# Value products of two attention stages: a head's high and low value parts side by side as one stationary, and rows of exponentials divided by their sums

## The chip, the cores and the metric

The kernel runs on one core of a Trainium2 chip. The metric is device time in microseconds of that core; lower is better. A profile adds one execution seen by the hardware profiler, with every instruction on the five engines: TensorE (PE, whose weight loads stand apart as PEld), VectorE (DVE), ScalarE (ACT), GpSimd (POOL) and SyncE (SP), which issues the transfers.

## What is computed

A causal decoder trunk of two layers on 512 tokens of width 1024, in float32. Layer 0 mixes with 4 differential heads and 8 dilated heads; layer 1 mixes with 16 heads that see only keys picked by an indexer. Each layer then has a squared-ReLU MLP and a gated embedding. The change touches the last step of the dilated heads and of layer 1's heads, which in the reference is

```
pr = jnp.exp(s - lse[..., None])
o = jnp.einsum('bhcnqk,bhcnkd->bhcnqd', pr.astype(v.dtype), vv)
...
pr = jax.nn.softmax(jnp.where(valid[:, :, None, :], s, -jnp.inf), axis=-1)
o_lat = jnp.einsum('bqhk,bqkc->bqhc', pr.astype(sel.dtype), sel[..., :C_KV_RANK])
return jnp.einsum('bqhc,chd->bqhd', o_lat, w_uv)
```

The kernel applies `w_uv` to the keys' latent first, so that a head of layer 1 has values of 64 columns, as the dilated heads have.

## The kernel before

To keep float32 accuracy every operand of a product is split into a high part, which TensorE takes exactly, and a low part (the difference). A product is then three passes, `mm3` (L203): high by high, high by low, low by high. TensorE follows the order of the program; the other engines' orders come from a scheduler.

Both attention stages run through `head_pipe` (L404), a software pipeline over heads. Per step it issues four stages for different heads, in the order of `ORDER_B` for the dilated heads ("stage B" below, 8 heads) and `ORDER_C` for layer 1 ("stage C", 16 heads). In C, step i does A for head i+3, B for i+2, C for i and D for i-1:

- A transposes queries (tile `trq`, L381).
- B computes scores in four query tiles of 128, 256, 384 and 512 keys (tile `sc`), takes row maxima on VectorE (L346), exponentials with row sums on ScalarE (L347), written to the head's tile `p` (`pb` or `pc`, 128x1280). For the second head of a pair it takes reciprocals of the pair's eight sums (L424) and spreads them along rows (tile `rsb`). At its end the next pair's keys are split (`k_load`, tile `kc`: high part on VectorE, low part on GpSimd, L1131).
- C transposes ten 128x128 blocks of `p` (tile `trp`, L361) and splits them into a high (ScalarE, L364) and a low part (VectorE, L365).
- D is the product (tile `pv`, `pv_head` L368). The stationary of a matmul is the 128 value columns of a pair of heads, so half of the 128 output rows belong to the other head and are not used. Six groups of blocks (`GRP`) times three passes are 18 matmuls. For the first head of a pair it also transposes `rsb` on TensorE (tile `rs`, L439, four transposes) and ScalarE copies it to `rbp` (L441). VectorE multiplies product and `rbp` into the tile `on` (L446). After the second head, `on` is split into the output's high part (ScalarE) and low part (L450: GpSimd in B, VectorE in C). After the first head, the values of the next pair are split in C (`v_pair`, tile `vhl`, low part on GpSimd, L1148).

In stage B pieces of other products (`ple`, and `pj` of the output projection) follow the steps; in stage C only the last steps have such pieces. After each stage the output projection (`out_proj`, tile `pj`) goes on; its fourth piece needs the last pair's output. Scores and products share four PSUM banks (tag A).

```
    def mm3(ps, aH, aL, bH, bL, first, last):
        mm(ps, aH, bH, first, False)
        mm(ps, aH, bL, False, False)
        mm(ps, aL, bH, False, last)
```

Of the kernel before, what the change touches and what calls it, by code (L numbers as in the profile page):

```python
# [18 lines left out]
P = 128  # L19
# [16 lines left out]
# how the phases are woven: how much other work of the tensor engine follows a step of a  # L36
# pipeline, the heads that each of its stages runs ahead, the order of chunks
# [10 lines left out]
# engines: low parts of weight units (v: VectorE, p: GpSimd); spread sums, products'  # L48
# low and high parts; values' and keys' parts
# [3 lines left out]
ENG_B = ("act", "pool", "act")  # L53
ENG_C = ("pool", "vec", "act")
# [4 lines left out]
def trunk_kernel(ctx, tc, A, out):  # L59
# [3 lines left out]
    # the tensor engine runs in the order of the program  # L63
# [34 lines left out]
    # the activation functions' table is loaded before the first data come  # L98
# [5 lines left out]
    # row statistics: short-lived columns go round, kept ones stay  # L104
# [109 lines left out]
    # rows (128) of an activation in two parts, transposed: per k tile a slice  # L214
# [89 lines left out]
    # post-norm of y (two psum halves) added to the residual row tile r  # L304
# [14 lines left out]
    # pre-norm statistics of h (row tile r): 1/rms into rstd[:, r]  # L319
# [31 lines left out]
    # P (rows, per q tile at OFF) transposed into two parts, blocks ordered for the  # L351
    # products: q tiles (0,1): k0 q0 q1, k1 q1; q tiles (2,3): k0..k2 q2 q3, k3 q3
# [34 lines left out]
    def scores(qp, kk):  # L387
        """scores of the four q tiles, the first two in one bank."""
# [15 lines left out]
    def head_pipe(small, n, order, on, stA, kk, bias, scale, vHL, oHL, ptile, ptT, slack=0.0, end=0.0, done=None, scored=None):  # L404
# [3 lines left out]
        sums, inv = [None], {}  # L408
# [25 lines left out]
        def st_d(h):  # L434
            m = h % 2
            if m == 0:
                pr = bank("B", "rs")
                for qt in range(NR):
                    pe.transpose(pr[:, qt * P : (qt + 1) * P], inv[h + 1][:, qt].rearrange("p m d -> p (m d)"), ident)  # L439
                o[0] = small("rbp", h // 2), small("on", h // 2)  # L440
                act.copy(o[0][0], pr)  # L441
            rb, t = o[0]
            rows = slice(64 * m, 64 * m + 64)
            ps = bank("A", "pv")
            pv_head(ps, *vHL(h), *tr[h])
            vec.tensor_tensor(t[rows], ps[rows], rb[rows], op=ALU.mult)  # L446
            if m:
                oH, oL = oHL(h)
                cp(on[2], oH, t)
# [11 lines left out]
    def ple_proj(i, stage):  # L461
        """half of the projected embedding of layer i, through stage tiles to DRAM."""
# [18 lines left out]
    def rope_rows(mp, ps, n, half, cs, dst, leng):  # L481
        """dst = rotated ps; ps [128, n] viewed as heads of 2*half columns."""
# [12 lines left out]
    def rope32(mp, pv, heads, cs, dst, e=pool):  # L495
        """dst = rotated pv; pv [128, heads, 32]; dst the same, or [128, heads/2, 2, 32]."""
# [13 lines left out]
    def out_proj(oT):  # L510
        """the first columns of a mixer's output; its first three pieces need not the last heads."""
# [11 lines left out]
    with tc.tile_pool(name="att0", bufs=1) as mp:  # L523
# [11 lines left out]
        # chunk order: ak aq av bk bq bv (columns of w_in_ab are aq ak av bq bk bv)  # L535
# [9 lines left out]
        # first chunk: all row tiles at once, as the k tiles arrive  # L545
# [6 lines left out]
        # the tensor engine's clock comes up while the first loads are under way  # L552
# [27 lines left out]
        # statistics of x, rotation tables scaled by them  # L580
# [15 lines left out]
        # lambda  # L596
# [12 lines left out]
        # av: [kt][head, part, 128]  # L609
# [12 lines left out]
        # --- A: differential attention  # L622
# [93 lines left out]
        # --- B projections  # L716
        bk, evk = rope_evac("bk")
        bq, evq = rope_evac("bq")
        bvH = slot(5, "bvH", F32R).rearrange("p (k d) -> p k d", d=512)
        bvL = slot(9, "bvL", F32R).rearrange("p (k d) -> p k d", d=512)  # L720

        def bv_evac(r, ps):
            act.activation(bvH[:, r, :], ps, AF.Identity, scale=rstd0[:, r : r + 1])
            vec.scalar_tensor_tensor(bvL[:, r, :], ps, rstd0[:, r : r + 1], f32(bvH[:, r, :]), op0=ALU.mult, op1=ALU.subtract)
# [12 lines left out]
        # --- B: the three branches as one softmax over keys with multiplicities  # L737
# [18 lines left out]
        def small_b(nm, pr):  # L756
            return s3[:, {"rsb": pr % 2, "rbp": 2, "on": 3}[nm]]

        def v_b(h):
            c = slice(h // 2 * P, h // 2 * P + P)  # L760
            return lambda kt: bvH[:, kt, c], lambda kt: bvL[:, kt, c]
# [3 lines left out]
        weave(head_pipe(small_b, 8, ORDER_B, ENG_B, st_a, lambda h: ksets[h // 2 % 2][h % 2], lambda qt: mB[:, S - (qt + 1) * P :], SCALE_AB,  # L765
                        v_b, lambda h: (oTH[1][:, h // 2, :], oTL[1][:, h // 2, :]),
                        lambda h: (slot(1, "pb"), s4)[h % 4 - 2] if h % 4 >= 2 else mp.tile([P, 1280], F32, tag="p", bufs=2, name="pb"),
                        lambda h: pt_pair(mp, (12, 13) if h % 2 else None, f"pb{h}"), B_SLACK, B_END),
              itertools.chain(ple_proj(0, lambda q: stg[:, q % 4, :]), itertools.islice(og, 3)))
# [20 lines left out]
            # hidden layer, transposed  # L790
# [48 lines left out]
            # the projected embedding  # L839
# [3 lines left out]
            # second MLP product  # L843
# [38 lines left out]
            # gate  # L882
# [47 lines left out]
    def begin(xn):  # L930
        # the next mixer's first two row tiles, while the last one is normalised
# [6 lines left out]
    # =========================================================================  # L938
    # layer 1 mixer
    # =========================================================================  # L940
    with ExitStack() as ctx2:
# [8 lines left out]
        with tc.tile_pool(name="idx", bufs=1) as ip:  # L950
# [13 lines left out]
            def latent(ps, r, n, j, g):  # L964
                """rows of a normed latent; the transposes come later."""
# [13 lines left out]
            # queries' latent  # L979
# [11 lines left out]
            # keys' latent, rotated key, indexer key and weights  # L991
# [52 lines left out]
            # indexer queries (q tiles 1..3; the first keeps all its keys)  # L1044
# [43 lines left out]
            def queries():  # L1088
# [15 lines left out]
                # keys without the rotated part, transposed, a pair of heads each  # L1104
# [34 lines left out]
        # values of a pair of heads  # L1139
        vhl = slot(11, "vhl", F32R).rearrange("p (b t k d) -> p b t k d", b=2, t=2, k=NR)  # L1140
# [113 lines left out]
```

## Time and profile before

| | us |
|---|---|
| median of 3 runs | 1360.66 (1360.48 to 1360.87) |
| span of the profiled execution, first to last instruction | 1359.8 |
| PE busy in the span | 1342.1 (99%) |
| DVE / ACT / POOL busy | 711.0 (52%) / 576.0 (42%) / 262.4 (19%) |
| mean granted clock of TensorE | 0.997 of full speed |

The profiled execution has no time of its own beside its span; the median of the runs is 0.9 us above that span. The shares are means over a kernel with very different stages: stage B lies at about 190 to 243 us of the span, stage C at 813 to 914 us. PE at 99% says that TensorE seldom stands still, not that it is at its peak.

### The profile page before, as it was taken

The page shows a single profiled execution, that of the slowest core. Times are in us where ns is not written, and L with a number is a line of the kernel's source. Part 1 is how long each engine was busy: PE and PEld are TensorE (multiplying, and loading weights), DVE is VectorE, ACT ScalarE, POOL GpSimd, SP SyncE. Part 2 cuts the span into 40 slices and gives each one's busy share as a digit, 9 for nine tenths or more (in the row PEclk, how much of TensorE's full clock was granted, in tenths as well). Part 3 has the DMA queues.
Part 4 walks back from the last instruction along what each step waited for, and adds up shares of the span by engine and source line. Part 5 has one row for each costly group of instructions (what it writes and reads, how often), then busy time and mean ns, then how long its engine had stood idle before and what let it go on. Part 6 is the DMA issues. An engine that isn't in the chain of part 4 may idle for free.

```text
span 1359.8 us, 17867 instructions
## 1 busy us (share of the span) xinstructions
PE 1342.1 (99%) x6809; PEld 1129.8 (83%) x6809; DVE 711.0 (52%) x1297; ACT 576.0 (42%) x1113; POOL 262.4 (19%) x233
## 2 busy tenths in 40 slices
PE   9999999999999999999998999999999999999998
PEld 6888889888888888888897679998988888888887
DVE  6567677374333322225567998965633332222263
ACT  4244577244222322233355768854432223222332
POOL 4202101032000022222012753410400001222120
PEclk9999999999999999999999999999999999999999
DMA  7312131423333423332243331011432334333321
GB/s 287 106 62 71 62 117 55 155 98 120 93 103 99 155 93 98 103 94 77 94 150 101 109 112 44 1 62 64 133 100 93 95 105 157 93 93 99 103 77 48
DMA packets 40838, 135.39 MB, mean 100 GB/s; under 512 B 4656, under 2 KB 5808, under 8 KB 40752
## 3 DMA queue, kind: packets, MB, share of 16 engines
q1 hardware_dynamic: 40752, 134.24, 30.7%
q8 instruction: 54, 0.88, 0.3%
q14 instruction: 32, 0.26, 0.1%
HBM read 125.83 MB, written 8.39 MB: 99 GB/s over the span
## 4 chain that ended last, share of the span: by engine, by line
PE 89%; DVE 7%; POOL 2%; issue 1%; DMA 1%; ACT 0%; SPq 0%; POOLq 0%; DVEq 0%; ACTq 0%
PE z L201 26%; PE y L201 26%; PE pj L201 21%; PE sc L201 5%; PE pv L201 4%; PE trp L361 2%; DVE work L1085 2%; DVE m L1084 2%; PE ple L201 1%; PE ak L201 1%; POOL wl L141 1%; PE tr L242 1%; PE trq L381 1%; DVE wl L141 1%; PE pva L201 1%
## 5 line engine op out<-in xcount | busy, mean ns | idle before, releaser
L141 DVE TENSOR_TENSOR wl<-raw,wh 128x1024 fp32r<-128x1024 f32 (+3 forms) x190 | 250.4, 1322 | 276.1 <-ACT wh L137 273.9
L137 ACT CAST wh<-raw 128x1024 fp32r<-128x1024 f32 (+3 forms) x206 | 212.2, 1033 | 282.5 <-issue 184.8
L201 PE MATMUL y<-wh,ah 128*128 128x512 f32 x512 | 199.5, 390 | 0.0
L201 PE MATMUL y<-wh,al 128*128 128x512 f32 x512 | 199.2, 389 | 0.0
L201 PE MATMUL y<-wl,ah 128*128 128x512 f32 x512 | 199.2, 389 | 0.0
L201 PE MATMUL pj<-wh,big 128*128 128x512 f32 (+1 forms) x444 | 148.5, 386 | 0.0
L808 DVE SCALAR_TENSOR_TENSOR t<-z,rb 128x512 f32<-128x512 f32 x64 | 44.2, 691 | 187.2 <-PE z L201 187.2
L201 PEld LDWEIGHTS y<-wh,al 128*128 128x128 f32 x512 | 96.1, 188 | 20.0
L201 PEld LDWEIGHTS y<-wl,ah 128*128 128x128 f32 x512 | 96.1, 188 | 19.9
L201 PEld LDWEIGHTS y<-wh,ah 128*128 128x128 f32 x512 | 96.1, 188 | 19.7
L863 POOL TENSOR_TENSOR al<-big,ah 128x512 fp32r<-128x512 f32 x24 | 32.6, 1360 | 383.8 <-ACT ah L862 383.8
L201 PE MATMUL z<-hz1H,wl 128*128 128x512 f32 (+1 forms) x288 | 105.3, 366 | 0.6 <-DVE wl L141 0.6
L201 PE MATMUL z<-hz0H,wl 128*128 128x512 f32 (+1 forms) x288 | 105.3, 366 | 0.6 <-DVE wl L141 0.6
L201 PE MATMUL z<-hz1H,wh 128*128 128x512 f32 (+1 forms) x288 | 105.5, 366 | 0.2 <-ACT hz1H L248 0.2
L201 PE MATMUL z<-hz0H,wh 128*128 128x512 f32 (+1 forms) x288 | 105.5, 366 | 0.2 <-ACT hz0H L248 0.2
L201 PE MATMUL z<-hz0L,wh 128*128 128x512 f32 (+1 forms) x288 | 105.3, 366 | 0.3 <-DVE hz0L L249 0.3
L201 PE MATMUL z<-hz1L,wh 128*128 128x512 f32 (+1 forms) x288 | 105.3, 366 | 0.3 <-DVE hz1L L249 0.3
L201 PEld LDWEIGHTS pj<-wh,big 128*128 128x128 f32 x444 | 82.9, 188 | 18.9 <-issue 2.2
L862 ACT CAST ah<-a 128x512 fp32r<-128x512 f32 x40 | 24.8, 621 | 154.6 <-PE y L201 154.6
L863 POOL TENSOR_TENSOR al<-a,ah 128x512 fp32r<-128x512 f32 x40 | 51.7, 1293 | 165.9 <-ACT ah L862 165.9
L209 POOL TENSOR_TENSOR st<-st,mhalf 128x1 f32<-128x1 f32 (+1 forms) x41 | 27.6, 674 | 226.9 <-DVE st L312 115.8
L201 PEld LDWEIGHTS z<-hz1H,wl 128*128 128x128 f32 x288 | 54.3, 189 | 9.7 <-DVE wl L141 0.8
(598 smaller groups left out, 2687.2 us busy)
## 6 DMA issues: line engine op xcount, KB each, us to landing
raw<-in_w_mi_dram SPq DMA_DIRECT2D x64, 512.0 KB, 3.7
raw<-in_w_mo_dram SPq DMA_DIRECT2D x64, 512.0 KB, 3.6
raw<-in_w_ab_dram SPq DMA_DIRECT2D x20, 512.0 KB, 4.8
raw<-in_w_g_dram SPq DMA_DIRECT2D x16, 512.0 KB, 3.6
raw<-in_w_oab_dram SPq DMA_DIRECT2D x8, 512.0 KB, 4.3
ple<-ple_dram SPq DMA_DIRECT2D x8, 512.0 KB, 5.4
raw<-in_w_oc_dram SPq DMA_DIRECT2D x8, 512.0 KB, 3.6
xr<-in_x_dram SPq DMA_DIRECT2D x4, 512.0 KB, 9.5
```

The lines of the kernel that those rows point to most:

```text
L137: act.copy(h[:, :n], raw[:, :n])
L141: (pool if e == "p" else vec).tensor_tensor(l[:, c], raw[:, c], f32(h[:, c]), op=ALU.subtract)
L201: pe.matmul(ps, a, b, start=first, stop=last, skip_group_check=True)
L209: pool.tensor_tensor(dst, src, mhalf[:, :n], op=ALU.pow)
L242: pe.transpose(ps[:, i * P : (i + 1) * P], src(k), ident)
L361: pe.transpose(ps[:, i * P : (i + 1) * P], pt[:, OFF[qt] + kt * P : OFF[qt] + (kt + 1) * P], ident)
L381: pe.transpose(ps[:, r * P : (r + 1) * P], rows(r), ident)
L808: vec.scalar_tensor_tensor(t, ps, 0.0, rb, op0=ALU.max, op1=ALU.mult)
L862: act.copy(ah, src)
L863: pool.tensor_tensor(al, src, f32(ah), op=ALU.subtract)
L1084: vec.max(m8, w)
L1085: vec.match_replace(w, m8, w, MARK)
```

## The change

1. The values of a head are stored as [high 64 | low 64] (tiles `bv`, `vhl`), so one stationary holds both parts of one head, and the 128 output rows are (high part's product, low part's product). `pv_head` then needs two passes, with the high and the low part of the transposed exponentials: 12 matmuls.
2. The two halves of the output are added: ScalarE copies the low half into `on`, shifted to the head's 64 partitions, and VectorE adds the high half.
3. `rsb`, `rs` and `rbp` are gone. Each head takes reciprocals of its own four sums and GpSimd multiplies the four stretches of `p` by them, in place, before the transposes.
4. The low part of the output in stage C goes from VectorE to GpSimd (`ENG_C`), and C's `p` has three buffers in place of two. `on` has one buffer in C, as before.

```diff
-ENG_B = ("act", "pool", "act")
-ENG_C = ("pool", "vec", "act")
+ENG_B = ("act", "pool")
+ENG_C = ("act", "pool")
...
-    def pv_head(ps, vH, vL, th, tl):
+    def pv_head(ps, v, th, tl):
         for kt, b, q, w in GRP:
             o = ps[:, q * P : (q + w) * P]
-            ph, pl = th[:, b * P : (b + w) * P], tl[:, b * P : (b + w) * P]
-            mm3(o, vH(kt), vL(kt), ph, pl, b == 0, (kt == 1 and q == 1) or kt == 3)
+            mm(o, v(kt), th[:, b * P : (b + w) * P], b == 0, False)
+            mm(o, v(kt), tl[:, b * P : (b + w) * P], False, (kt == 1 and q == 1) or kt == 3)
...
-            nmx = stat(4)
-            if h % 2 == 0:
-                sums[0] = stat(8)
-            sm = sums[0][:, 4 * (h % 2) : 4 * (h % 2) + 4]
+            nmx, sm, rs = stat(4), stat(4), stat(4)
...
-            if h % 2:
-                rs = stat(8)
-                vec.reciprocal(rs, sums[0])
-                inv[h] = small("rsb", h // 2).rearrange("p (q m d) -> p q m d", q=NR, m=2)
-                cp(on[0], inv[h], rs.rearrange("p (m q) -> p q m", m=2).unsqueeze(3).to_broadcast([P, NR, 2, 64]))
+            vec.reciprocal(rs, sm)
+            for qt in range(NR):
+                c = slice(OFF[qt], OFF[qt] + (qt + 1) * P)
+                pool.tensor_scalar(t[:, c], t[:, c], rs[:, qt : qt + 1], None, op0=ALU.mult)
...
-                pr = bank("B", "rs")
-                for qt in range(NR):
-                    pe.transpose(pr[:, qt * P : (qt + 1) * P], inv[h + 1][:, qt].rearrange("p m d -> p (m d)"), ident)
-                o[0] = small("rbp", h // 2), small("on", h // 2)
-                act.copy(o[0][0], pr)
-            rb, t = o[0]
-            rows = slice(64 * m, 64 * m + 64)
+                o[0] = otile(h // 2)
+            t = o[0]
+            rows, rest = slice(64 * m, 64 * m + 64), slice(64 - 64 * m, 128 - 64 * m)
             ps = bank("A", "pv")
-            pv_head(ps, *vHL(h), *tr[h])
-            vec.tensor_tensor(t[rows], ps[rows], rb[rows], op=ALU.mult)
+            pv_head(ps, v(h), *tr[h])
+            act.copy(t[rows], ps[rest])
+            vec.tensor_tensor(t[rows], ps[rows], t[rows], op=ALU.add)
...
-                        lambda h: mp.tile([P, 1280], F32, tag="p", bufs=2, name="pc"), pt_c, 0.0, C_END,
+                        lambda h: mp.tile([P, 1280], F32, tag="p", bufs=3, name="pc"),
+                        lambda pr: mp.tile([P, S], F32, tag="on", bufs=1, name="on"), pt_c, 0.0, C_END,
```

TensorE in stage C, the first head of a pair: transposes of head 9's `p` (`trp`) and head 8's product (`pc8H`, `pc8L` are its transposed exponentials). Before:

```order
L361 MATMUL trp<-ident,pc 128x128 x10
L439 MATMUL rs<-ident,rsb 128x128 x4
L201 MATMUL pv<-pc8H,vhl 128x256
L201 MATMUL pv<-pc8L,vhl 128x256
L201 MATMUL pv<-pc8H,vhl 128x256
L201 MATMUL pv<-pc8H,vhl 128x128
L201 MATMUL pv<-pc8L,vhl 128x128
L201 MATMUL pv<-pc8H,vhl 128x128
```

With the change, the same place:

```order
L361 MATMUL trp<-ident,pc 128x128 x10
L201 MATMUL pv<-pc8H,vhl 128x256
L201 MATMUL pv<-pc8L,vhl 128x256
L201 MATMUL pv<-pc8H,vhl 128x128
L201 MATMUL pv<-pc8L,vhl 128x128
L201 MATMUL pv<-pc8H,vhl 128x256
```

Each of the six groups loses its third matmul, and the four transposes of `rs` are gone.

GpSimd in stage C, one pair of heads. Before (low parts of two keys, the spread sums, low parts of values):

```order
L1131 TENSOR_TENSOR kc<-kn_6005,kc 64x512
L73 COPY rsb<-st 128x512
L1131 TENSOR_TENSOR kc<-kn_6005,kc 64x512
L1148 TENSOR_TENSOR vhl<-v_5554,vhl 128x256
L1148 TENSOR_TENSOR vhl<-v_5555,vhl 128x256
```

With the change, also one pair:

```order
L1120 TENSOR_TENSOR kc<-kn_5973,kc 64x512
L421 TENSOR_SCALAR pc<-pc,st 128x128
L421 TENSOR_SCALAR pc<-pc,st 128x256
L421 TENSOR_SCALAR pc<-pc,st 128x384
L421 TENSOR_SCALAR pc<-pc,st 128x512
L1120 TENSOR_TENSOR kc<-kn_5973,kc 64x512
L421 TENSOR_SCALAR pc<-pc,st 128x128
L421 TENSOR_SCALAR pc<-pc,st 128x256
L421 TENSOR_SCALAR pc<-pc,st 128x384
L421 TENSOR_SCALAR pc<-pc,st 128x512
L1137 TENSOR_TENSOR vhl<-v_5522,vhl 128x4x64
L1137 TENSOR_TENSOR vhl<-v_5523,vhl 128x4x64
```

The next row there is `L442`, the low part of the output (tile `oc`). So the pair has eight multiplications and one subtraction more, and no copy; a head's multiplications stand two steps ahead of the transposes that read them.

ScalarE in stage C with the change, from the copy of head 6's product to the exponentials of head 10, with waits:

```order
L437 COPY on<-pv 64x512 [waits PE_49,Pool_49]
L384 CAST qc11H<-trq 128x512 [waits PE_49]
L364 CAST pc8H<-trp 128x512 [waits PE_49]
L347 ACTIVATE pc,st<-pc,st 128x128 [waits DVE_49]
L347 ACTIVATE pc,st<-pc,st 128x256 [waits DVE_49]
```

The copy of a pair's first head writes the single tile `on`, and so waits for GpSimd's L442 of the pair before, which stands in GpSimd's queue behind a later head's multiplications and the next values; queries and exponentials are queued behind the copy.

## Rows read from the trace of the kernel before

**Rows 1.** Busy time by engine in stage C and stage B (PE, PEld, DVE, ACT, POOL, clock)
```profile
840.00:885.80 45.80, 45.80 (x370) 44.35 (x368) 43.27 (x121) 39.35 (x113) 18.64 (x20) 1.00 0.07 24
198.50:236.10 37.60, 37.60 (x273) 33.75 (x271) 26.32 (x66) 28.37 (x74) 3.85 (x3) 1.00 0.15 54
```

**Rows 2.** Chain that ended last, stage B and its end: start us, us, what
```profile
198.69 0.44 PE rs L439 x4
199.12 2.05 PE pv L201 x18
...
240.53 0.70 DVE big L446
...
241.26 0.63 ACT oTbH L73
...
241.95 1.29 POOL oTbL L450
...
243.29 6.87 PE pj L201 x29
```

**Rows 3.** The same chain in stage C
```profile
863.16 2.05 PE pv L201 x18
...
874.63 2.05 PE pv L201 x18
...
903.97 1.09 PE trp L361 x10
905.50 2.05 PE pv L201 x18
907.55 1.42 PE pj L201 x6
```

**Rows 4.** Timeline of PE in one product of stage C, in part
```profile
863.41 0.28 PE L201 MATMUL pv<-pc6L,vhl 128*128 128x128 f32 x1
863.53 0.44 PE L201 MATMUL pv<-pc6H,vhl 128*128 128x128 f32 x2
863.81 0.28 PE L201 MATMUL pv<-pc6L,vhl 128*128 128x256 f32 x1
863.92 0.40 PE L201 MATMUL pv<-pc6H,vhl 128*128 128x256 f32 x2
864.16 0.28 PE L201 MATMUL pv<-pc6L,vhl 128*128 128x256 f32 x1
```

**Rows 5.** Groups of GpSimd by form, whole span: busy us, mean ns
```profile
L1131 POOL TENSOR_TENSOR kc<-kn,kc 64x512 fp32r<-64x512 f32 x16 | 20.6, 1288 | 32.7 <-DVE kc L73 21.8 <-PE sc L201 11.0
...
L1080 POOL TENSOR_TENSOR work<-rl,work 128x384 f32<-128x384 f32 x7 | 7.1, 1013 | 3.3 <-ACT rl L1079 3.0
...
L450 POOL TENSOR_TENSOR oTbL<-big,oTbH 128x512 fp32r<-128x512 f32 x4 | 5.1, 1287 | 67.5 <-ACT oTbH L73 67.5
...
L73 POOL COPY rsb<-st 128x512 f32<-128x512 f32 x8 | 5.0, 623 | 15.7 <-DVE st L424 15.5
```

**Rows 6.** GpSimd's lines L593 and L1148: duration ns min/median/max
```profile
L593 POOL TENSOR_SCALAR cs<-cs,st x4: 522/524/1439, 24.4 to 26.8; 128x96 f32<-128x96 f32 x4
...
L1148 POOL TENSOR_TENSOR vhl<-v,vhl x16: 727/735/1457, 795.9 to 895.6; 128x256 fp32r<-128x256 f32 x16
```

**Rows 7.** Timeline of GpSimd and VectorE at the start of stage C
```profile
819.56 1.30 POOL L1131 TENSOR_TENSOR kc<-kn,kc 64x512 fp32r<-64x512 f32 x1 [10.99 <-PE sc L201]
...
822.40 1.28 POOL L1131 TENSOR_TENSOR kc<-kn,kc 64x512 fp32r<-64x512 f32 x1 [1.54 <-DVE kc L73]
...
821.84 0.42 DVE L73 CAST kc<-kn 64x512 fp32r<-64x512 f32 x1
...
823.33 0.64 DVE L73 CAST kc<-kn 64x512 fp32r<-64x512 f32 x1
```

**Rows 8.** Groups of VectorE and ScalarE by form, 840 to 885.8 us
```profile
L450 DVE TENSOR_TENSOR oc<-on,oc 128x512 fp32r<-128x512 f32 x5 | 4.0, 802 | 0.7
...
L441 ACT COPY rbp<-rs 128x512 f32<-128x512 f32 x4 | 2.5, 618 | 0.0
```

More of the change, by code (lines that the diff above doesn't have):

```diff
@@ L402, in pt_pair, with head_pipe @@
                 mp.tile([P, 1280], F32R, tag="ptl", bufs=1, name=name + "L"))
-    def head_pipe(small, n, order, on, stA, kk, bias, scale, vHL, oHL, ptile, ptT, slack=0.0, end=0.0, done=None, scored=None):
+    def head_pipe(n, order, on, stA, kk, bias, scale, v, oHL, ptile, otile, ptT, slack=0.0, end=0.0, done=None, scored=None):
         q, p, tr, o = {}, {}, {}, [None]
-        sums, inv = [None], {}
         def st_a(h):
@@ L436, in st_d @@
             if m == 0:
-                pr = bank("B", "rs")
-                for qt in range(NR):
-                    pe.transpose(pr[:, qt * P : (qt + 1) * P], inv[h + 1][:, qt].rearrange("p m d -> p (m d)"), ident)
-                o[0] = small("rbp", h // 2), small("on", h // 2)
-                act.copy(o[0][0], pr)
-            rb, t = o[0]
-            rows = slice(64 * m, 64 * m + 64)
+                o[0] = otile(h // 2)
+            t = o[0]
+            rows, rest = slice(64 * m, 64 * m + 64), slice(64 - 64 * m, 128 - 64 * m)
             ps = bank("A", "pv")
-            pv_head(ps, *vHL(h), *tr[h])
-            vec.tensor_tensor(t[rows], ps[rows], rb[rows], op=ALU.mult)
+            pv_head(ps, v(h), *tr[h])
+            act.copy(t[rows], ps[rest])
+            vec.tensor_tensor(t[rows], ps[rows], t[rows], op=ALU.add)
             if m:
                 oH, oL = oHL(h)
-                cp(on[2], oH, t)
+                cp(on[0], oH, t)
                 eng[on[1]].tensor_tensor(oL, t, f32(oH), op=ALU.subtract)
@@ L718, in trunk_kernel @@
         bq, evq = rope_evac("bq")
-        bvH = slot(5, "bvH", F32R).rearrange("p (k d) -> p k d", d=512)
-        bvL = slot(9, "bvL", F32R).rearrange("p (k d) -> p k d", d=512)
+        bvt = [slot((5, 9)[q], f"bv{q}", F32R).rearrange("p (k h t d) -> p k h t d", k=2, t=2, d=64) for q in range(2)]
         def bv_evac(r, ps):
-            act.activation(bvH[:, r, :], ps, AF.Identity, scale=rstd0[:, r : r + 1])
-            vec.scalar_tensor_tensor(bvL[:, r, :], ps, rstd0[:, r : r + 1], f32(bvH[:, r, :]), op0=ALU.mult, op1=ALU.subtract)
+            hi, lo = (bvt[r // 2][:, r % 2, :, t, :] for t in range(2))
+            ps = ps.rearrange("p (h d) -> p h d", d=64)
+            act.activation(hi, ps, AF.Identity, scale=rstd0[:, r : r + 1])
+            vec.scalar_tensor_tensor(lo, ps, rstd0[:, r : r + 1], f32(hi), op0=ALU.mult, op1=ALU.subtract)
         def fill_b():
@@ L754, in trunk_kernel @@
         s3 = slot(3, "small").rearrange("p (a s) -> p a s", s=S)
-        def small_b(nm, pr):
-            return s3[:, {"rsb": pr % 2, "rbp": 2, "on": 3}[nm]]
         def v_b(h):
-            c = slice(h // 2 * P, h // 2 * P + P)
-            return lambda kt: bvH[:, kt, c], lambda kt: bvL[:, kt, c]
+            return lambda kt: bvt[kt // 2][:, kt % 2, h].rearrange("p t d -> p (t d)")
         oT = XT(([(oTH[k // 4], k % 4) for k in range(8)], [(oTL[k // 4], k % 4) for k in range(8)]))
         p0, og = out_proj(oT)
-        weave(head_pipe(small_b, 8, ORDER_B, ENG_B, st_a, lambda h: ksets[h // 2 % 2][h % 2], lambda qt: mB[:, S - (qt + 1) * P :], SCALE_AB,
+        weave(head_pipe(8, ORDER_B, ENG_B, st_a, lambda h: ksets[h // 2 % 2][h % 2], lambda qt: mB[:, S - (qt + 1) * P :], SCALE_AB,
                         v_b, lambda h: (oTH[1][:, h // 2, :], oTL[1][:, h // 2, :]),
                         lambda h: (slot(1, "pb"), s4)[h % 4 - 2] if h % 4 >= 2 else mp.tile([P, 1280], F32, tag="p", bufs=2, name="pb"),
-                        lambda h: pt_pair(mp, (12, 13) if h % 2 else None, f"pb{h}"), B_SLACK, B_END),
+                        lambda pr: s3[:, pr % 2], lambda h: pt_pair(mp, (12, 13) if h % 2 else None, f"pb{h}"), B_SLACK, B_END),
               itertools.chain(ple_proj(0, lambda q: stg[:, q % 4, :]), itertools.islice(og, 3)))
@@ L1137, in st_a @@
             return q_pair(mp, lambda r: qrow[:, r, a : a + P], f"qc{h}")
-        vhl = slot(11, "vhl", F32R).rearrange("p (b t k d) -> p b t k d", b=2, t=2, k=NR)
+        vhl = slot(11, "vhl", F32R).rearrange("p (b k m t d) -> p b k m t d", b=2, k=NR, m=2, t=2)
         def v_pair(pr):
@@ L1144, in v_pair @@
             for q in range(2):
-                src, k = vrow[q][:, :, c], slice(2 * q, 2 * q + 2)
-                vh, vl = (vhl[:, pr % 2, t, k] for t in range(2))
+                src = vrow[q][:, :, c].rearrange("p k (m d) -> p k m d", d=64)
+                vh, vl = (vhl[:, pr % 2, 2 * q : 2 * q + 2, :, t, :] for t in range(2))
                 cp(VH_C, vh, src)
@@ L1150, in v_c @@
         def v_c(h):
-            v = vhl[:, h // 2 % 2]
-            return lambda kt: v[:, 0, kt, :], lambda kt: v[:, 1, kt, :]
+            return lambda kt: vhl[:, h // 2 % 2, kt, h % 2].rearrange("p t d -> p (t d)")
         def pt_c(h):
@@ L1161, in trunk_kernel @@
         p0, og = out_proj(oT)
-        weave(head_pipe(lambda nm, pr: mp.tile([P, S], F32, tag=nm, bufs=2 if nm == "rsb" else 1, name=nm), 16, ORDER_C, ENG_C, st_a, lambda h: kset[h % 2], lambda qt: biast[:, OFF[qt] : OFF[qt] + (qt + 1) * P], SCALE_C,
+        weave(head_pipe(16, ORDER_C, ENG_C, st_a, lambda h: kset[h % 2], lambda qt: biast[:, OFF[qt] : OFF[qt] + (qt + 1) * P], SCALE_C,
                         v_c, lambda h: (oTs[0][h // 8][:, h // 2 % 4, :], oTs[1][h // 8][:, h // 2 % 4, :]),
-                        lambda h: mp.tile([P, 1280], F32, tag="p", bufs=2, name="pc"), pt_c, 0.0, C_END,
+                        lambda h: mp.tile([P, 1280], F32, tag="p", bufs=3, name="pc"),
+                        lambda pr: mp.tile([P, S], F32, tag="on", bufs=1, name="on"), pt_c, 0.0, C_END,
                         done=lambda h: v_pair(h // 2 + 1) if h % 2 == 0 and h < 14 else None,
```

## The prediction

> **What bounds the kernel now.** I read three views in this order. First the busy time by engine in the two stages that the change touches. In stage C (840 to 885.8 us) TensorE is busy all 45.8 us at full clock, but VectorE is busy 43.27 and ScalarE 39.35 of them, GpSimd only 18.64; in stage B TensorE is again busy without a break (37.6 of 37.6), VectorE and ScalarE at 70 to 75% and GpSimd at 10% [rows 1]. So TensorE sets the pace in both, and in C two engines stand close behind it. Second the chain of waits: through both stages it runs along TensorE, with a product of 18 matmuls at 2.05 us and, once per pair, four transposes of the spread sums at 0.44 us [rows 2, 3]. From one product to the same one a pair later C takes 874.63 - 863.16 = 11.47 us [rows 3]. Third the timeline inside a product: matmuls on 128 columns are spaced like those on 256, 863.41 to 863.81 being 0.13 each and 863.92 to 864.16 being 0.12 each [rows 4]. The pace is per matmul, not per column, so dropping one of three passes pays for short ones too.
>
> **What TensorE loses.** 2.05 / 18 = 0.114 us a matmul; six fewer a head is 0.68 us; a pair loses 2 x 0.68 + 0.44 = 1.80 us. Twelve pairs give 21.6 us: 7.2 in B (4 pairs), 14.4 in C (8 pairs). This much leaves the path only if no other engine becomes the slower one.
>
> **What the other engines gain and lose, per pair of C.** ScalarE: 39.35 / 45.8 x 11.47 = 9.9 us busy now [rows 1]; the copy of `rbp` (0.62) goes [rows 8], two copies of a product's half come, on 512 columns also, so at most 0.62 each: 10.5. VectorE: 43.27 / 45.8 x 11.47 = 10.8; the low part of the output (0.80) goes [rows 8], a second short reciprocal comes (some 0.2): 10.2. The product's multiply becomes an add of the same shape: nothing. TensorE: 11.47 - 1.80 = 9.7. Already these would leave C only about 1 of its 1.80 us.
>
> GpSimd is the question. Kept: two low parts of keys at 1.288 [rows 5] and two of values at 0.735 [rows 6]. Added: one low part of the output, priced by stage B's row at 1.287 [rows 5]. Together 5.33 us a pair. Then come two heads times four multiplications on 128, 256, 384 and 512 columns, 1280 in all. The only row of such an instruction is on 96 columns, 0.522 us [rows 6]. How much of that is fixed must be bounded from its neighbours. Subtractions on 384 and 512 columns take 1.013 and 1.287, so 2.14 ns a column over 0.19 fixed; the copy takes 0.623 on 512 [rows 5], with the same fixed part 0.85 ns a column.
>
> - Lower end: the multiplication grows like the copy, which also reads one tensor. Fixed 0.522 - 96 x 0.00085 = 0.44; a head takes 4 x 0.44 + 1280 x 0.00085 = 2.85 us.
> - Upper end: it grows like the subtraction. Fixed 0.317; a head takes 1.27 + 2.74 = 4.0 us.
>
> I take 2.9, next to the copy, because the multiplication reads one tensor and one column. GpSimd then needs 5.33 + 5.8 = 11.1 us a pair, more than any other engine and almost the old 11.47: in C GpSimd replaces TensorE as the bound.
>
> The Trainium skill (GPSIMD Engine Reference, section 4.1) speaks against this place: it sends elementwise multiplication to VectorE and calls GpSimd some two times slower for two inputs, but roughly at line rate for one. Line rate at that page's 1.2 GHz would be an estimate of 2.86 us a head, beside my 2.9, and the sum would come out 0.6 us lower; on 96 columns the trace shows 0.522, far from line rate, so the fixed part decides.
>
> A second cost is a collision with VectorE's copies of the keys' high parts. Alone such a copy took 0.42; the one that started at 823.33, while GpSimd was at work (822.40 + 1.28), took 0.64 [rows 7]. I charge GpSimd 0.2 us for each, 0.4 a pair. (The Trainium skill, SBUF — State Buffer, section "Who interferes with whom", says that a VectorE copy in a two-port mode and GpSimd exclude each other; the longer row agrees.) Below, nothing; above, a whole wait of a multiplication, near 0.8, for each.
>
> **The sum for stage C.** GpSimd ends its first low part of the next keys at 819.56 + 1.30 = 820.9 [rows 7], and the first head's multiplications can follow. From there to the last head's it does 16 heads x 2.9 = 46.4, 13 low parts of keys = 16.7, 12 of values = 8.8, six of outputs = 7.7, and 7 x 0.4 = 2.8 of collisions: 82.4, so it ends at 903.3. Then six of the last head's ten transposes remain, 6 x 1.09 / 10 = 0.65: they end at 903.9, against 903.97 + 1.09 = 905.1 now [rows 3]: -1.1. Behind them stand two products and one `rs` less work: -(2 x 0.68 + 0.44) = -1.8. At the end the chain from product to the output's low part is copy 0.62, add 0.70, cast 0.63, GpSimd 1.29, with gaps some 3.3 us. The projection can do six matmuls, three of the next pair's and two more meanwhile, 11 x 1.42 / 6 = 2.6 [rows 2, 3, 8]: +0.7. Stage C: -2.2.
>
> **The sum for stage B.** GpSimd needs 2 x 2.9 + 1.29 = 7.1 us a pair there, well under what TensorE keeps, and the multiplications have a whole step of cover before the transposes. ScalarE loses two copies a pair (of the sums, and `rbp`) and gains two: nothing. So TensorE's 7.2 stay, less 0.6 for the longer chain at the end, where TensorE waits for GpSimd already (241.95 + 1.29, then the projection goes on at 243.29 [rows 2]) and a copy of 0.62 is put ahead, and less 0.6 for small waits: -6.0. Between +0 and -7.2 everything is possible; full cover makes the far end likelier.
>
> The stored layout of the values and the third buffer of `p` cost nothing: the same instructions on the same columns, in runs of 64.
>
> Sum: -6.0 - 2.2 = -8.2. The span, 1359.8, becomes 1351.6; the median of the runs lies 0.9 above it, so I forecast **1352.5 us**. With multiplications at 2.85, no collisions and B whole it is 1347.5; with twice the collisions and 0.1 us more a head it is 1357.
>
> **The rivals.**
>
> *The multiplications grow like subtractions* (slower). Place: GpSimd's queue in C. At 4.0 us a head GpSimd needs 13.3 us a pair; the last transposes end 16 x 1.1 = 17.6 us later than above, at 921.5, which is +16.4; C is +15.3, B still -6.0: 1370. The turn is where C loses 6.0, at 2.9 + 8.2 / 16 = 3.4 us a head, about 1.5 ns a column. For it: every two-input row of GpSimd grows at 2.14. Against: the copy. A second way here is the single buffer of `on`: ScalarE's copy of a pair's first half waits for GpSimd's low part of the last pair, with exponentials queued behind; each 0.9 us a pair that GpSimd then stands idle costs 6 us.
>
> *A draw.* Between 3.25 and 3.55 us a head C loses what B gains: 1360.7. The middle of the two ends, 3.43, lies here.
>
> *The fixed part is not fixed.* If GpSimd overlaps it from one multiplication to the next and only 0.19 remains, a head takes 4 x 0.19 + 1.09 = 1.85 and GpSimd 9.4 us a pair; then ScalarE at 10.5 sets C, 1 us a pair less for 7 pairs, -7.9 with the end: 1346.8. Against: the 0.522 is from multiplications in a row.
>
> *TensorE's whole 21.6 us come off* (1339). Against: ScalarE's and VectorE's 10.5 and 10.2 over TensorE's 9.7. That the change does not do what it says is no case: the instruction order shows 12 matmuls a head where 18 were.
>
> **How the numbers follow.** A measurement of this kernel tells about 0.2%, 2.7 us, from no change. Chances: forecast 0.47, draw 0.18, slow multiplications or waits around them 0.25, overlapped fixed part 0.08, all of TensorE's gain 0.02. Faster is 0.47 + 0.08 + 0.02 = 0.57, same 0.18, slower 0.25. The likeliest case alone spans 1347.5 to 1357. For 8 in 10 the range goes from 1346, which takes in most of the overlapped case, to 1369, which leaves out the upper half of the slow one.
>
> **What would show it.** In stage C GpSimd busy over 90%, a head's four multiplications at 2.9 us, TensorE with gaps of around 0.9 us a head ended by GpSimd at the transposes, and a pair at 11.1 to 11.5 us. In stage B a pair shorter by 1.5 to 1.8 us with TensorE still unbroken. Products of 12 matmuls at 1.37 us. It is wrong if the multiplication on 512 columns is far from 0.9 us, if C's pair falls under 10.8 us, or if stage B does not shrink.

## The result, and the profile after

The changed kernel takes 1374.89 us (median of 4 runs, 1373.94 to 1375.63) where the kernel before, run beside it, takes 1360.76 (1360.48 to 1361.7): a ratio of 1.01, 95% interval 1.0086 to 1.0115. It is slower by 14 us; 1352.5 had been forecast, and the time lies above the whole range. The profiled span is 1372.8 us.

The busy time by engine in the same two stretches as [rows 1] (PE, PEld, DVE, ACT, POOL, granted clock):

```profile
840.00:885.80 45.80, 36.58 (x235) 34.35 (x234) 31.46 (x90) 31.32 (x87) 45.27 (x44) 0.85 0.06 24
198.50:236.10 37.60, 37.10 (x251) 31.94 (x249) 28.11 (x72) 30.52 (x77) 28.23 (x26) 1.00 0.22 71
```

In stage C GpSimd is busy 45.27 of 45.8 us, where 18.64 stood, and TensorE, VectorE and ScalarE all have gaps. In stage B TensorE still works almost without a break. So the two stages have gone different ways. Stage B ends in the chain of waits thus (start us, us, what):

```profile
230.95 2.77 PE pv L201 x24
...
235.78 1.28 POOL oTbL L442
...
237.11 8.01 PE pj L201 x34
```

The output projection gets its last low part and goes on at 237.11, against 243.29 in [rows 2]: 6.2 us earlier. A product of 12 matmuls takes 2.77 / 2 = 1.39 us. Stage C's chain, one pair of heads of it:

```profile
871.36 1.22 POOL oc L442
...
872.66 1.27 POOL kc L1120
...
874.02 3.16 POOL pc L421 x4
...
878.53 0.85 POOL kc L1120
...
879.79 2.56 POOL pc L421 x3
...
882.61 1.56 POOL pc L421
884.17 1.40 POOL vhl L1137 x2
885.57 1.23 POOL oc L442
```

The chain has left TensorE for GpSimd. From one low part of the output to the next it is 885.57 - 871.36 = 14.2 us, where a pair took 11.47 [rows 3]. The groups of GpSimd by form, 800 to 935 us (busy us, mean ns of one):

```profile
L421 POOL TENSOR_SCALAR pc<-pc,st 128x512 f32<-128x512 f32 x16 | 26.1, 1633 | 0.0
L421 POOL TENSOR_SCALAR pc<-pc,st 128x384 f32<-128x384 f32 x16 | 20.5, 1284 | 0.0
L1120 POOL TENSOR_TENSOR kc<-kn,kc 64x512 fp32r<-64x512 f32 x16 | 20.4, 1276 | 15.1 <-ACT qc2H L384 9.6 <-DVE kc L73 5.0
L421 POOL TENSOR_SCALAR pc<-pc,st 128x256 f32<-128x256 f32 x16 | 14.8, 923 | 0.0
L421 POOL TENSOR_SCALAR pc<-pc,st 128x128 f32<-128x128 f32 x16 | 10.3, 643 | 0.7
```

A head's four multiplications take 1.63 + 1.28 + 0.92 + 0.64 = 4.48 us, started one behind the other; 2.9 had been forecast, and 4.0 as the upper end. Two heads of them, two low parts of keys (1.28), two of values (0.72) and one of the output (1.27) are 14.2 us: the pair, to the tenth. GpSimd's timeline of one pair, the last head's multiplications, and VectorE's copy of the keys' high part that falls beside the first of them:

```profile
874.02 4.54 POOL L421 TENSOR_SCALAR pc<-pc,st 128x128 f32<-128x128 f32 x4
...
879.79 4.38 POOL L421 TENSOR_SCALAR pc<-pc,st 128x128 f32<-128x128 f32 x4
...
913.53 4.29 POOL L421 TENSOR_SCALAR pc<-pc,st 128x128 f32<-128x128 f32 x4
```

```profile
876.69 0.43 DVE L73 CAST kc<-kn 64x512 fp32r<-64x512 f32 x1
```

Who waits in 840 to 886 us (us in total, times, longest):

```profile
ACT on L437 <- POOL oc L442: 11.7, 3, 5.2
...
PE pv L201 <- DVE on L438: 8.6, 3, 3.0
PE trp L361 <- POOL pc L421: 0.7, 1, 0.7
```

These rows point elsewhere: most of the waiting is not at the transposes, which read the multiplied rows, but at the only buffer `on`, which ScalarE may not overwrite before GpSimd has subtracted; TensorE's products stand behind. So the trace allows two theories. **T1**: GpSimd's work sets the pace, and the waits are only where it shows. **T2**: the single buffer `on` sets it. TensorE's clock is a third suspect, at 0.85 in this stretch.

### The profile page after: what moved, and what is told of

Its sections match the earlier page's. It is cut to its first block, busy times and chain, and to the rows that moved or that the text cites. A ratio compares the mean times of both kernels' runs of the same rounds, so it can differ in the third digit from the quotient of the medians.

```text
span 1372.8 us, 17595 instructions
## 1 busy us (share of the span) xinstructions
PE 1332.2 (97%) x6617; PEld 1115.1 (81%) x6617; DVE 708.4 (52%) x1301; ACT 581.7 (42%) x1121; POOL 373.0 (27%) x329
## 4 chain that ended last, share of the span: by engine, by line
PE 78%; POOL 8%; DVE 8%; issue 3%; ACT 2%; DMA 1%; SPq 0%; POOLq 0%; DVEq 0%; ACTq 0%
PE z L201 26%; PE y L201 25%; PE pj L201 19%; POOL pc L421 3%; PE sc L201 2%; DVE work L1074 2%; DVE m L1073 2%; PE ak L201 1%; DVE wl L141 1%; POOL wl L141 1%; PE tr L242 1%; PE pv L201 1%; PE ple L201 1%; PE trp L361 1%; PE pva L201 1%
## 5 line engine op out<-in xcount | busy, mean ns | idle before, releaser
L201 PEld LDWEIGHTS y<-wh,ah 128*128 128x128 f32 x512 | 96.1, 188 | 19.9
L421 POOL TENSOR_SCALAR pc<-pc,st 128x128 f32<-128x128 f32 (+1 forms) x64 | 70.6, 1121 | 0.7
```

The lines of the kernel that those rows point to most:

```text
L201: pe.matmul(ps, a, b, start=first, stop=last, skip_group_check=True)
L421: pool.tensor_scalar(t[:, c], t[:, c], rs[:, qt : qt + 1], None, op0=ALU.mult)
```

## The experiments

Each ratio is to the kernel before, run on the same chip; as that took 1359.56 to 1361.78 us there, rows are best compared by their ratios. "Pair" is stage C's, from one GpSimd or ScalarE row of the output to the next pair's.

| run | us | ratio (95% interval) | pair, us |
|---|---|---|---|
| the change | 1374.89 | 1.0100 (1.0086 to 1.0115) | 14.2 |
| e1 stage B alone | 1354.99 | 0.9959 (0.9943 to 0.9975) | as before |
| e2 two `on` buffers | 1374.09 | 1.0099 (1.0083 to 1.0115) | 13.9 |
| e3 no multiplications in C | 1350.40 | 0.9931 (0.9911 to 0.9950) | 11.0 |
| e4 two-tensor multiplications | 1361.05 | 1.0001 (0.9991 to 1.0011) | 12.5 |
| e5 e4, keys' parts by maximum | 1363.99 | 1.0015 (1.0005 to 1.0024) | 12.8 |
| e6 C divides the products | 1362.12 | 1.0008 (0.9999 to 1.0017) | 12.5 |
| e7 e6, values on GpSimd | 1358.63 | 0.9980 (0.9971 to 0.9990) | 12.1 |
| e8 e7, keys' parts by maximum | 1359.85 | 0.9994 (0.9984 to 1.0003) | 12.3 |
| e9 e6, outputs on GpSimd | 1358.22 | 0.9992 (0.9982 to 1.0001) | 12.7 |
| e10 e9, values on GpSimd | 1350.24 | 0.9929 (0.9914 to 0.9944) | 11.2 |
| e11 e4, keys' parts on ScalarE | 1353.83 | 0.9955 (0.9940 to 0.9970) | 11.65 |
| e12 e10, sums later | 1356.44 | 0.9965 (0.9952 to 0.9978) | 12.4 |

**e1, stage B alone.** Stage C gets the functions and layouts of before.

```diff
-ENG_C = ("act", "pool")
+ENG_C = ("pool", "vec", "act")
...
-        vhl = slot(11, "vhl", F32R).rearrange("p (b k m t d) -> p b k m t d", b=2, k=NR, m=2, t=2)
+        vhl = slot(11, "vhl", F32R).rearrange("p (b t k d) -> p b t k d", b=2, t=2, k=NR)
```

> The change in the dilated heads alone (stage B); the layer 1 heads (stage C) are those of before. Both theories: B keeps its 6.2 us and C gives nothing back, 1360.7 - 6.2 = 1354.5 us, at most 1 us of it given back where later work waits for a load. If B's gain were given back later (a third theory, that the stages are not independent), 1359 or more. Stage C's pair 11.4 to 11.6 us as before.

Measured 1354.99, 6.0 us under its kernel before. Stage B's gain stays whole, and the difference to the change, 1374.89 - 1354.99 = 19.9 us, is stage C's loss.

**e2, two buffers `on` in stage C.** A third tile of exponentials and the second `on` take the slot of the odd heads' transposed rows, which get a tile of their own.

```diff
+        def on_c(pr):
+            return s0[:, 1280:1792] if pr % 2 else mp.tile([P, S], F32, tag="on", bufs=1, name="on")
...
-                        lambda pr: mp.tile([P, S], F32, tag="on", bufs=1, name="on"), pt_c, 0.0, C_END,
...
+                        on_c, pt_c, 0.0, C_END,
```

> The change with two buffers for the sum of a product's halves (`on`) in stage C. T1 (the throughput of GpSimd sets C's pace: 2 x 4.45 us of multiplications, 2 x 1.28 and 2 x 0.77 of low parts of keys and values, 1.27 of outputs, 14.2 us a pair): the pair stays at 13.9 to 14.3 us, GpSimd over 96% busy, total 1373 to 1376. T2 (ScalarE's copy, which waits for GpSimd's subtraction on the only buffer, with the products queued behind, sets it): the pair falls to 10.5 to 12 us, total 1350 to 1358.

Measured 1374.09, a pair of 13.9 us. ScalarE no longer waits for L442 there, and the time has moved by about 1 us (0.8 by the medians, 1.1 when each is set against its own kernel before). The kernel's busy time by engine in the stretch of the first view, and GpSimd's groups on `pc` (busy us, mean ns):

```profile
840.00:885.80 45.80, 35.11 (x257) 31.12 (x255) 39.56 (x103) 35.31 (x99) 45.19 (x44) 1.00 0.07 24
```

```profile
L421 POOL TENSOR_SCALAR pc<-pc,st 128x512 f32<-128x512 f32 x11 | 17.2, 1565 | 0.0
L421 POOL TENSOR_SCALAR pc<-pc,st 128x384 f32<-128x384 f32 x11 | 13.9, 1261 | 0.0
L421 POOL TENSOR_SCALAR pc<-pc,st 128x256 f32<-128x256 f32 x11 | 10.5, 957 | 0.0
...
L421 POOL TENSOR_SCALAR pc<-pc,st 128x128 f32<-128x128 f32 x11 | 6.7, 609 | 0.5
```

GpSimd is as dense as before. The clock is 1.00 here, 0.85 in the change, at nearly the same pair: T2 falls, and the clock as a cause with it. The waits at `on`, up to 5.2 us long, were worth about 1 us, less than the runs' own spread of 1.7 to 2.1 us.

**e3, no multiplications in stage C.** `div` is false for stage C, so this kernel leaves out the division by the sums there.

```diff
-            for qt in range(NR):
+            for qt in range(NR if div else 0):
```

> The change without the 64 multiplications of GpSimd in stage C: there the rows of exponentials are not divided by their sums. T1: GpSimd falls to 5.3 us a pair, and the pair to what ScalarE or TensorE needs, 10.3 to 10.9 us; total 1346 to 1351. T2: the wait for the one buffer stays; the pair stays above 12 us, total 1362 or more.

Measured 1350.40, a pair of 11.0 us, with `on` still single. The 64 multiplications of stage C cost 1374.89 - 1350.40 = 24.5 us. T1 holds, T2 falls again. Without them the rest of the change in C is worth 1354.99 - 1350.40 = 4.6 us. The busy time by engine in stage C:

```profile
843.00:886.00 43.00, 40.85 (x295) 35.52 (x293) 40.64 (x116) 40.39 (x114) 19.23 (x19) 1.00 0.07 26
```

Three engines are at 94 to 95% here. So 11.0 should be near the floor of this way of sharing the work out.

**e4, the multiplication as an operation of two tensors.**

```diff
-                pool.tensor_scalar(t[:, c], t[:, c], rs[:, qt : qt + 1], None, op0=ALU.mult)
+                pool.tensor_tensor(t[:, c], t[:, c], rs[:, qt : qt + 1].to_broadcast([P, (qt + 1) * P]), op=ALU.mult)
```

> The change with each multiplication of GpSimd as an operation of two tensors, the reciprocals spread along the columns. If it costs what the subtractions cost (0.19 us + 2.14 ns a column): 0.46, 0.74, 1.01 and 1.29 us on 128 to 512 columns, 3.5 us a head where 4.45 were. T1: 16 x 0.95 = 15 us less, total 1359 to 1361, pair 12.2 to 12.5 us. T2: under half of that, 1368 or more. If an operand without a stride is read no faster than a scalar: 1374 to 1376.

GpSimd's groups in stage C (busy us, mean ns):

```profile
L421 POOL TENSOR_TENSOR pc<-pc,st 128x512 f32<-128x512 f32 x16 | 17.0, 1060 | 0.0
L421 POOL TENSOR_TENSOR pc<-pc,st 128x384 f32<-128x384 f32 x16 | 13.2, 824 | 0.0
...
L421 POOL TENSOR_TENSOR pc<-pc,st 128x256 f32<-128x256 f32 x16 | 9.8, 611 | 0.0
...
L421 POOL TENSOR_TENSOR pc<-pc,st 128x128 f32<-128x128 f32 x16 | 6.4, 397 | 2.2 <-DVE st L418 1.7
```

The same product is cheaper with two tensors than with a tensor and a column: 2.89 us a head by these means, cheaper than expected, and the price that the forecast had taken. Yet the total is 1361.05 and not 1352.5. That T1's 1359 to 1361 was all but met is luck: its price of 3.5 us a head was too high, and waits that it did not have made up for it. GpSimd's work is 2 x 2.75 (four multiplications in a row of its timeline) + 2.56 + 1.42 + 1.28 = 10.8 us a pair; the pair takes 12.5. The timelines of GpSimd and VectorE around one copy of the keys' high parts (start us, us, what, and in brackets the wait before it):

```profile
856.58 1.29 POOL L1120 TENSOR_TENSOR kc<-kn,kc 64x512 fp32r<-64x512 f32 x1 [1.34 <-DVE kc L73]
...
860.54 1.42 POOL L1137 TENSOR_TENSOR vhl<-v,vhl 128x256 fp32r<-128x256 f32 x2
...
861.93 1.28 POOL L442 TENSOR_TENSOR oc<-on,oc 128x512 fp32r<-128x512 f32 x1
...
863.67 1.27 POOL L1120 TENSOR_TENSOR kc<-kn,kc 64x512 fp32r<-64x512 f32 x1 [0.46 <-DVE kc L73]
```

```profile
856.03 0.40 DVE L73 CAST kc<-kn 64x512 fp32r<-64x512 f32 x1
...
861.03 2.47 DVE L73 CAST kc<-kn 64x512 fp32r<-64x512 f32 x1
863.53 0.69 DVE L365 TENSOR_TENSOR ptL<-trp,ptH 128x512 fp32r<-128x512 f32 x1
```

With GpSimd idle the copy takes 0.40. The one at 861.03 takes 2.47: it ends 0.29 us after GpSimd's run of subtractions does (861.93 + 1.28 = 863.21). VectorE's queue stands for 2 us, the other keys' copy is late in turn, and GpSimd, which subtracts that copy, waits for it: 1.34 + 0.46 = 1.8 us a pair, the difference between 12.5 and 10.8. Its waits in 843 to 886 us (us in total, times, longest):

```profile
POOL kc L1120 <- DVE kc L73: 6.7, 7, 1.3
```

**e5, the keys' high parts by another operation.** The copy becomes the larger of a tensor and itself, to see whether its form matters.

```diff
-                cp(KH_C, h[a : a + 64], src[a : a + 64])
+                vec.tensor_tensor(h[a : a + 64], src[a : a + 64], src[a : a + 64], op=ALU.max)
```

> The run e4 with one more edit: VectorE writes the keys' high parts as the larger of a tensor and itself (a two-input operation, 0.69 us on 512 columns like its other ones) and not as a copy. T4 (in e4 the pair of 12.54 us is GpSimd's 10.7 us of work and 1.8 us of its waits for VectorE's copies, which take up to 2.46 us in place of 0.42 while GpSimd runs without a break): the operation takes 0.69 wherever it falls, the pair comes to 11.0 to 11.7 us (all four engines need 10 to 11), total 1350 to 1356. Rival (the copies only wait for something else that comes late, such as the keys' buffer): the operation takes as long as the copy took, the pair stays at 12.4 or more, total 1360 or more.

A miss for T4: the time rose to 1363.99. In the timeline of VectorE:

```profile
873.71 3.00 DVE L1119 TENSOR_TENSOR kc<-kn 64x512 fp32r<-64x512 f32 x1
876.73 0.69 DVE L365 TENSOR_TENSOR ptL<-trp,ptH 128x512 fp32r<-128x512 f32 x1
```

The new operation is held as well, for longer (it takes 0.67 where GpSimd stands idle). L365, which reads one of its tensors from PSUM, the memory that TensorE writes its products to, takes at most 0.69 everywhere. The expectation had taken that row for the rule of all two-input operations; here both operands lie in SBUF, the memory that holds the tiles. Whether it was held by GpSimd or waited for something else, this run could not say; e11 could.

**e11, the copies of the keys on ScalarE.**

```diff
-VH_C, VL_C, KH_C, KL_C = "act", "pool", "vec", "pool"
+VH_C, VL_C, KH_C, KL_C = "act", "pool", "act", "pool"
```

> The run e4 (multiplications as operations of two tensors, 2.75 us a head) with the copies of the keys' high parts on ScalarE in place of VectorE. T5 (VectorE's operations whose operands all lie in SBUF are held while GpSimd works on two tensors, and GpSimd's next low part waits for them): nothing of VectorE is held any more; GpSimd is no longer idle for 1.8 us a pair, ScalarE needs 10.7 + 2 x 0.6 = 11.9; pair 11.9 to 12.2 us, total 1355 to 1359. Rival (in e4 and e5 the keys' copies wait for something else): the copies on ScalarE are late as well, pair 12.5 or more, total 1361 or more.

The copies of the keys on ScalarE in 840 to 886 us (duration ns, min/median/max), and the busy time by engine:

```profile
L73 ACT CAST kc<-kn x7: 616/617/617, 843.8 to 878.8; 64x512 fp32r<-64x512 f32 x7
```

```profile
843.00:886.00 43.00, 37.95 (x279) 33.59 (x280) 34.41 (x106) 42.32 (x114) 39.83 (x49) 1.00 0.04 14
```

1353.83, with a pair of 11.65 (a little better than T5's 11.9). Each set against its own kernel before, that is some 6 us better than e4. All seven copies take 0.617 us beside a GpSimd that is busy 39.83 of 43 us; its waits for the keys' copies are gone, and ScalarE, at 42.32 of 43, is now the bound. That is T5's picture, and its rival is out.

**e6 to e10 and e12, a better stage C.** Stage B stays as changed. Stage C keeps the two passes, but the spread, transposed sums of a pair divide once, behind the sum of the halves:

```diff
-            pv_head(ps, *vHL(h), *tr[h])
-            vec.tensor_tensor(t[rows], ps[rows], rb[rows], op=ALU.mult)
+            pv_head2(ps, vHL(h), *tr[h])
+            act.copy(t[rows], ps[rest])
+            vec.tensor_tensor(t[rows], ps[rows], t[rows], op=ALU.add)
             if m:
+                pool.tensor_tensor(t, t, rb, op=ALU.mult)
                 oH, oL = oHL(h)
```

> Stage B as changed. In stage C two passes with the stacked values, but the sums of a pair divide the sum of the product's halves as before the change (spread, transposed, copied to `rbp`, GpSimd multiplies once a pair). GpSimd needs 7.2 us a pair, ScalarE 10.9 to 11.0, VectorE 10.4, TensorE 10.1. T1: the pair is 11.0 to 11.6 us, set by ScalarE; total 1351 to 1356. T2: the one `on` buffer, now held by two operations of GpSimd, stops ScalarE: pair 12 or more, total over 1360.

1362.12, a miss for T1; time and pair are those of T2, but by another wait. In the chain of waits (start us, us, what) it is not the buffer that stops ScalarE: the copy of the output's high part, on ScalarE, stands behind GpSimd's multiplication (1.28 us), and the next exponentials behind it. Scores, products and the next multiplication follow from these, so that the waits close into a ring:

```profile
844.59 0.59 ACT on L456
...
845.20 0.71 DVE on L457
...
846.04 1.28 POOL on L459
...
847.34 0.62 ACT oc L73
```

e7 moves the values' high parts to GpSimd; e8 adds e5's edit to e7.

```diff
-VH_C, VL_C, KH_C, KL_C = "act", "pool", "vec", "pool"
+VH_C, VL_C, KH_C, KL_C = "pool", "pool", "vec", "pool"
```

> The run e6 with the values' high parts on GpSimd in place of ScalarE: ScalarE 10.3, GpSimd 8.1 us a pair. If ScalarE sets e6's pace: pair 10.7 to 11.1 us, total 1347 to 1352. If VectorE's copies of the keys collide more with the longer GpSimd work: no better than e6.

> The run e7 with the keys' high parts as the larger of a tensor and itself, as in e5. The collisions go (up to 0.5 us a pair) and VectorE works 0.5 us a pair longer: within 2 us of e7. If it is much better, the collisions cost e7 time.

1358.63, better than e6 by 3.5 us but not by the 10 hoped for: the ring of e6 is still there. e8's 1359.85 lies within its 2 us.

e9 is e6 with the output's high part on GpSimd, so that ScalarE waits no more, and the last pair's steps on VectorE and ScalarE; e10 is e9 with e7's edit.

```diff
-ENG_C = ("pool", "pool", "act")
+ENG_C = ("pool", "pool", "pool")
...
-                pool.tensor_tensor(t, t, rb, op=ALU.mult)
+                last = h == n - 1
+                (vec if last else pool).tensor_tensor(t, t, rb, op=ALU.mult)
```

> The run e6 with the output's high part on GpSimd as well (a copy, 0.62 us), so that ScalarE no longer stands behind GpSimd's multiplication of a pair; for the last pair the three steps are on VectorE and ScalarE. GpSimd needs 7.8 us a pair, ScalarE 10.3, VectorE 10.4, TensorE 10.1. If the chain of e6 (product, copy, add, GpSimd's multiplication, ScalarE's high part, exponentials) set its pair of 12.5 us: pair 10.6 to 11.2 us, total 1348 to 1353, under stage B's change alone (1355.0). If GpSimd's longer runs hold VectorE's copies of the keys: pair 11.5 or more, total 1355 or more.

> The run e9 with the values' high parts on GpSimd too: ScalarE 9.7, GpSimd 8.7 us a pair. Pair 10.5 to 11.2 us, total 1347 to 1353; not better than e9 by over 1 us if VectorE (10.4) sets the pace, or worse if GpSimd's runs hold VectorE's copies.

e9 missed, at 1358.22: ScalarE's copy to the single `on` now waits for GpSimd's low part (1.8 us in 43), and that wait lies in its chain. The held copies that its expectation named are a small part (one a pair, 0.95 us, as long as in e6). e10 hit: 1350.24, the fastest kernel of the study, 0.71% under the kernel before (interval 0.56 to 0.86%). The busy time by engine:

```profile
843.00:886.00 43.00, 39.97 (x310) 37.31 (x309) 38.67 (x112) 39.09 (x106) 32.55 (x38) 1.00 0.07 25
```

No engine has over 93% of the stretch. Why the step from e9 to e10, 0.6 us less for ScalarE, is worth 8 us, was not taken apart. The timelines of GpSimd show this difference, among smaller ones: in e9 the next keys' low part (846.93, 1.28 us) stands between the output's high part (846.24) and its low part (848.29); in e10 it stands behind both (845.03, 845.86, then 847.23), and ScalarE no longer waits for `on`.

e12 moves the transposes of the sums and `rbp` to a pair's second product:

```diff
-            if m == 0:
+            if m:
                 pr = bank("B", "rs")
```

> The run e10 with the transposes of the spread sums and the copy to `rbp` moved from a pair's first product to its second, so that the copy to the only `rbp` no longer stands behind GpSimd's multiplication with the last pair's sums. If that wait (multiplication, four transposes, `rbp`, exponentials: one piece of e10's chain) sets its pair of 11.2 us: pair 10.5 to 10.9 us, total 1344 to 1348. If VectorE's and ScalarE's work in turn sets it: 11.0 or more, total 1349 to 1351.

1356.44, a pair of 12.4: slower than e10, and outside both totals expected. ScalarE now waits for `on` once a pair, behind GpSimd's four steps in a row (longest 0.6 us), among which the keys' low part stands before the output's again, as in e9. As the edit brought this wait along, the run does not settle whether the wait at `rbp` sets e10's pair. The three runs point to the order in which GpSimd gets its work, besides its sum; no run changed the order alone.

## Why the prediction was wrong

**Right: stage B.** -6.0 was forecast, the chain shows -6.2 and e1 measures -6.0. The step "TensorE's 7.2 stay, less 0.6 and 0.6" stands, with the 12-matmul product at 1.39 us (1.37 forecast). That it is met to the tenth is in part luck, as the 0.6 for small waits was a guess. It stands although the multiplications were underpriced there too: GpSimd is busy 28.23 of 37.6 us, and the cover was deep enough.

**Right: which engine becomes the bound of C**, GpSimd, and that TensorE's 14.4 us there mostly don't leave the path; but the pair is 14.2 us, not 11.1 to 11.5. e3 shows the most that this sharing of the work gives up with GpSimd out of the way: 4.6 us.

**Wrong: the price of the multiplication.** The failing step is "I take 2.9, next to the copy". Bounds had been drawn from other instructions' growth, 0.85 and 2.14 ns a column; the multiplication grows by (1565 - 609) / 384 = 2.5 ns a column over 0.29 us (e2's rows), faster than a subtraction of two tensors: 4.27 us a head in e2's timeline, and 4.3 to 4.5 in the change's. On 96 columns that gives 0.53, as [rows 6] had it. The one row had been consistent with the truth all along; the mistake was to take the two neighbours for ends of what is possible. The rival "the multiplications grow like subtractions" had the right place and sign, but 4.0 a head gave 1370.

Set into the forecast's own sum, four multiplications at the 4.27 of a head with no copy beside it put 16 x (4.27 - 2.9) = 21.9 us onto 1352.5: 1374.4, beside 1374.89 measured. So the queue's sum was right in form, and one term carried the miss. (The forecast's low end of 1347.5 adds up to 1347.7, which changes nothing.) The Trainium skill (GPSIMD Engine Reference, section 4.1), by which an operation of one input runs roughly at line rate, gave an estimate of 2.86 beside the choice (the sum gives 2.84); the change's 4.27 is far from it, and the measurement decides.

**Wrong in form, right in size by luck: the collisions.** 0.2 us each, 0.4 a pair, had been charged for VectorE's copies. In the change a copy falls beside each head's multiplications, which take 4.54 and 4.38 there against 4.27: 0.4 a pair. But in e4, where the multiplications do cost the 2.9 forecast, GpSimd waits 1.8 a pair for the copies and the time is 1361 and not 1352.5; e11, which takes the copies away from VectorE, gives 1353.8. [Rows 7] already held the pattern: the copy at 823.33 took 0.64, to 823.97, which is 0.29 us after GpSimd's end at 822.40 + 1.28 = 823.68, the same 0.29 as in e4. It had been read as a copy that runs slower; by the rows of e4 it was a copy that stands until GpSimd's subtraction is done, so its price depends on what GpSimd has queued. The bound named for it, 0.8 each, was too low as well: in e4 a copy is held 2.47 - 0.40 = 2.1 us.

**Not the cause**: the second way that the prediction named, the single buffer of `on`. It has the longest of TensorE's and ScalarE's waits in stage C, where the prediction had looked for TensorE's gaps at the transposes, and e2 prices them at about 1 us.

## What to carry to other kernels

A single row on 96 columns cannot price an instruction on 512: if its growth decides the sign, bounds taken from other operations are no bounds, and the forecast belongs on the side where the rows grow fastest. Where an engine is busy without a gap, the waits elsewhere are its shadow, however long: compare its work per round with the round before mending a buffer. And when a term is confirmed but the sum still misses, as in e4, look for what the next engine in the ring waits for.

## What the runs showed of the hardware

- GpSimd's multiplication of a tensor by a column (0.61, 0.96, 1.26, 1.57 us on 128 to 512 columns) is dearer than the same one as two tensors with the column spread (0.40, 0.61, 0.82, 1.06). The first row is e2's, the second e4's.
- VectorE's copy of the keys, which reads only SBUF, is held while GpSimd runs operations of two tensors: 2.47 us for 0.40 beside e4's subtractions, and 1.24 beside one of e4's multiplications of two tensors (816.84, ending 0.28 us behind that at 816.76 of 1.04). The maximum of two inputs in its place is held too (3.00 for 0.67 in e5). L365, which also reads PSUM, is not (at most 0.69), nor is ScalarE's copy (0.617), nor VectorE's reciprocal of four columns (0.17 at 851.60 of e4, beside L1120). The Trainium skill (SBUF — State Buffer, section "Who interferes with whom") names both held forms and says that ScalarE waits for nobody; the rows agree. It speaks of a block for one instruction. In e4 the copy at 861.03 stood until three of them were through, while in e5 one maximum came in between two, and then GpSimd's L442 took 1.80 in place of 1.27:

```profile
848.57 1.80 DVE L1119 TENSOR_TENSOR kc<-kn 64x512 fp32r<-64x512 f32 x1
```

```profile
848.35 1.43 POOL L1137 TENSOR_TENSOR vhl<-v,vhl 128x256 fp32r<-128x256 f32 x2
849.73 1.80 POOL L442 TENSOR_TENSOR oc<-on,oc 128x512 fp32r<-128x512 f32 x1
```

- GpSimd's multiplications by a column hold a copy little: 0.43 and 0.56 in the change's steady stretch, up to 0.71 in e2. In VectorE's timeline of e2 the first of these two copies fell beside L421, the second beside L1137 and L442:

```profile
862.29 0.69 DVE L73 CAST kc<-kn 64x512 fp32r<-64x512 f32 x1
870.17 1.81 DVE L73 CAST kc<-kn 64x512 fp32r<-64x512 f32 x1
```

- In the changed kernel TensorE's granted clock falls to half, its lower level of 1.2 GHz, after waits of 2.7 and 2.8 us for ScalarE's and VectorE's part of a product in stage C (before 859.78 and 873.97), and comes back; the busy time by engine, with the clock behind it:

```profile
873.00:880.00 7.00, 6.03 (x26) 6.04 (x27) 6.42 (x18) 6.45 (x18) 6.90 (x7) 0.52 0.00 0
880.00:887.00 7.00, 6.67 (x51) 6.02 (x50) 4.13 (x14) 3.83 (x13) 6.92 (x8) 0.99 0.00 1
```

In this kernel, where TensorE waits for GpSimd anyway, that cost little: e2, at full clock in the same stretch, takes about the same time.
